# Feed-forward gate and up products of a float32 network: pairs of feature blocks in seven block products instead of eight, and the down product in four groups

## The chip, the core and the metric

The kernel runs on one core of a Trainium2 chip. The metric is the device time of one launch in microseconds (us), median of several runs. Five engines work on their own instruction rows, each in order: PE (TensorE) multiplies matrices, DVE (VectorE) and ACT (ScalarE) do the element-wise work, POOL (GpSimd) takes some of it, and SP (SyncE) issues most DMA transfers. Engines wait for one another through semaphores.

## The reference

Two blocks of two layers each act on 512 tokens of 1024 features, in float32. What matters here is the feed-forward part at the end of each layer of the second block: a norm, two products to 2816 features (gate and up), a convolution over three tokens on the gate, silu, the product of both, and a product back to 1024 features.

```python
# first block, two layers: x = x + rms_norm(mixed(rms_norm(x)) @ w_out)
...
for l in range(DEPTH):
    hn = rmsnorm(h, norm_mix[l])
    if l % 2 == 0:
        h = h + even_mixer(hn, ...)
    else:
        h = h + odd_mixer(hn, ...)
    h = h + conv_ffn(rmsnorm(h, norm_ffn[l]), ffn_w_up[l], ffn_w_gate[l],
                     ffn_conv_w[l], ffn_conv_b[l], ffn_w_down[l])
return rmsnorm(h, norm_final)[:, N_META:N_META + S]

def conv_ffn(h, w_up, w_gate, conv_w, conv_b, w_down):
    u = h @ w_up
    g = h @ w_gate
    g = lax.conv_general_dilated(g, ...) + conv_b
    return (jax.nn.silu(g) * u) @ w_down
```

In layer 0 there are 528 tokens (16 meta tokens and 512 of x). In layer 1 only the 512 tokens of x are wanted, and for the gate 4 tokens ahead of them, 516 columns in all.

## The kernel before

Activations lie with features on partitions, in blocks (or chunks) of 128, and tokens in columns. A float32 product runs as three passes: weights and activations are each split exactly into a high and a low part, and `dense()` issues, for each chunk k of the contraction, high times high, high times low and low times high (L165). 528 columns take two PSUM banks, so each pass is two matmuls of 264 columns; 516 columns are two of 258.

`weights()` loads 512 KB or less by SP (tile `wr`, L148), copies the high part on ACT (`wh`, L149) and subtracts on DVE to get the low part (`wl`, L150). The pool holds 2 tiles `wr`, 4 `wh` and 4 `wl`. `split()` does the same to activations (L155, L156). `Norm.part` makes the operand of a norm's products: X times the gain, high on ACT (L68) and low on DVE (L69), and sums squares (L232, L235); the statistics of each token pass through PE (L242, `ps_ss`, and L259, `ps_rs`), and the result `rs` multiplies products as they leave PSUM.

`ffn()` goes through the 22 feature blocks in three groups of 8, 7 and 7. For a block it makes the gate product and the up product (8 chunks of contraction each, 48 matmuls each in layer 0; in layer 1 the up product is 24 matmuls of 512 columns). The gate takes `rs` on DVE as it leaves PSUM (tile `g`, L1077), then ACT (`z`, L1078), two convolution steps on DVE (L1080), silu on ACT (L1081), z times `rs` on POOL (L1082), z times the up product on DVE (L1083), and the split into `aH` and `aL`. After a group, `added()` multiplies its chunks with the down weights: for each of 8 output blocks one product of 7 or 8 chunks, added to X on DVE (L694). The last group of layer 1 goes through `final()`, which works by halves of the tokens and ends with the last norm and the output.

The program is written in this order; a scheduler that estimates times, and the limited tiles of each pool, set in what order each engine's instructions stand in the end. The row of each engine is then fixed and is worked off in order.

## Time and profile before

| | |
|---|---|
| median of three runs | 2132.17 us (2124.72, 2132.17, 2137.76) |
| profiled execution, its span | 2134.1 us |
| PE busy | 2066.6 us, 97% |
| DVE, ACT, POOL busy | 58%, 41%, 26% |
| feed-forward layer 0, unbroken matmuls | 380.94 us |
| feed-forward layer 1, unbroken matmuls | 337.98 us |

The profile is of one execution. Its own time is the span; nothing outside it is recorded for that execution. The feed-forward parts are some 34% of the span. A line number such as L165 is one of the kernel before; the changed kernel's lines are one higher up to `ffn()`, and its own from there on.

### The profile page before, as it was taken

How to read it: one execution, taken by the hardware profiler on the slowest of the kernel's cores; microseconds unless marked ns; L12 is line 12 of the kernel's file. 1: busy time of each engine (PE TensorE's matmuls, PEld its weight loads, DVE VectorE, ACT ScalarE, POOL GpSimd, SP SyncE). 2: the span in 40 equal slices, each digit the busy share in tenths (PEclk: the TensorE clock that was granted, in tenths of full speed). 3: DMA queues.
4: the chain of work that ended last, by engine and by line, in shares of the span. 5: the costliest groups of instructions: out<-in, count | busy, mean ns of one | idle time of the engine just before them, and what ended most of it. 6: DMA issues, size and time to landing. Idle time of an engine off the chain costs nothing.

```text
span 2134.1 us, 36059 instructions
## 1 busy us (share of the span) xinstructions
PE 2066.6 (97%) x14456; PEld 1888.8 (89%) x14456; DVE 1228.9 (58%) x2016; ACT 865.7 (41%) x1543; POOL 544.9 (26%) x652
## 2 busy tenths in 40 slices
PE   8999999999989999999999999999999999999998
PEld 6788888788789899988999999999888899888898
DVE  5565756665666896545554354454665665444454
ACT  5455644455644322344333232334433444223233
POOL 2222223222235555364010010001445401000001
PEclk9999999999999999999999999999999999999999
DMA  6633224633224323343222223234342233322322
GB/s 202 182 106 106 65 87 132 167 105 99 65 75 121 89 80 98 113 129 83 79 99 90 90 86 94 90 90 115 106 121 76 81 106 99 95 94 82 106 84 75
DMA packets 75590, 216.49 MB, mean 101 GB/s; under 512 B 10936, under 2 KB 15056, under 8 KB 75424
## 3 DMA queue, kind: packets, MB, share of 16 engines
q1 hardware_dynamic: 71792, 205.93, 33.3%
q0 software_dynamic: 2336, 7.19, 1.2%
q8 instruction: 114, 1.87, 0.4%
q10 hardware_dynamic: 1296, 1.09, 0.2%
q14 instruction: 52, 0.43, 0.1%
HBM read 166.20 MB, written 6.92 MB: 81 GB/s over the span
## 4 chain that ended last, share of the span: by engine, by line
PE 83%; DVE 7%; DMA 4%; issue 2%; SPq 1%; ACT 1%; POOL 1%; DVEq 0%; POOLq 0%; ACTq 0%
PE ps_mm L165 66%; PE ps_s L372 2%; PE ps_t L379 2%; PE ps_o L469 2%; PE ps_out L165 1%; DMA ks<-st 1%; PE ps_o L984 1%; PE ps_o L412 1%; PE ps_z L1034 1%; DVE yo L579 1%; DVE wl L150 1%; PE ps_t L956 1%; DMA sq<-t 1%; PE ps_ro L863 1%; DVE s L1037 1%
## 5 line engine op out<-in xcount | busy, mean ns | idle before, releaser
L165 PE MATMUL ps_mm<-hH,wh 128*128 128x264 f32 (+3 forms) x2712 | 677.0, 312 | 18.2 <-DVE t L189 7.5
L165 PE MATMUL ps_mm<-hL,wh 128*128 128x264 f32 (+3 forms) x2712 | 679.6, 311 | 10.8 <-DVE hL L69 10.8
L165 PE MATMUL ps_mm<-hH,wl 128*128 128x264 f32 (+3 forms) x2712 | 678.1, 311 | 0.0
L149 ACT ACTIVATE wh<-wr 128x1024 fp32r<-128x1024 f32 (+3 forms) x301 | 301.5, 1003 | 633.8 <-PE ps_mm L165 573.9
L165 PEld LDWEIGHTS ps_mm<-hH,wh 128*128 128x128 f32 x2712 | 448.6, 190 | 47.0 <-DVE t L189 7.7
L165 PEld LDWEIGHTS ps_mm<-hL,wh 128*128 128x128 f32 x2712 | 448.4, 190 | 35.7 <-DVE hL L69 12.5
L165 PEld LDWEIGHTS ps_mm<-hH,wl 128*128 128x128 f32 x2712 | 448.7, 190 | 25.6 <-issue 1.4
L150 DVE TENSOR_TENSOR wl<-wr,wh 128x1024 fp32r<-128x1024 f32 (+3 forms) x277 | 330.9, 1196 | 99.1 <-ACT wh L149 89.4
L1082 POOL TENSOR_TENSOR z<-z,rs 128x528 f32<-128x528 f32 (+1 forms) x44 | 58.1, 1322 | 601.6 <-ACT z L1081 601.6
L694 DVE TENSOR_TENSOR X<-X,ps_mm 128x528 f32<-128x528 f32 (+2 forms) x72 | 50.2, 697 | 156.1 <-PE ps_mm L165 155.7
L165 PE MATMUL ps_mm<-aL,wh 128*128 128x264 f32 (+2 forms) x528 | 134.4, 310 | 0.0
L165 PE MATMUL ps_mm<-aH,wl 128*128 128x264 f32 (+2 forms) x528 | 134.2, 309 | 0.0
L165 PE MATMUL ps_mm<-aH,wh 128*128 128x264 f32 (+2 forms) x528 | 133.9, 309 | 0.0
L189 DVE TENSOR_TENSOR t<-ps_mm,rs 128x528 f32<-128x528 f32 (+1 forms) x101 | 70.1, 695 | 85.1 <-PE ps_mm L165 79.6
L1077 DVE TENSOR_TENSOR g<-ps_mm,rs 128x528 f32<-128x528 f32 (+1 forms) x44 | 30.8, 701 | 119.9 <-PE ps_mm L165 119.9
L165 PE MATMUL ps_mm<-yH,wh 128*128 128x264 f32 (+2 forms) x392 | 95.3, 309 | 0.2 <-DVE X L694 0.2
L165 PE MATMUL ps_mm<-yH,wl 128*128 128x264 f32 (+2 forms) x392 | 94.6, 307 | 0.0
L165 PE MATMUL ps_mm<-yL,wh 128*128 128x264 f32 (+2 forms) x392 | 93.8, 305 | 0.0
L165 PEld LDWEIGHTS ps_mm<-aL,wh 128*128 128x128 f32 x528 | 87.6, 188 | 5.6
L165 PEld LDWEIGHTS ps_mm<-aH,wl 128*128 128x128 f32 x528 | 87.5, 188 | 5.5
L165 PEld LDWEIGHTS ps_mm<-aH,wh 128*128 128x128 f32 x528 | 87.2, 188 | 5.6
L1083 DVE TENSOR_TENSOR z<-z,ps_mm 128x528 f32<-128x528 f32 (+1 forms) x44 | 30.6, 695 | 87.8 <-PE ps_mm L165 48.6
(268 smaller groups left out, 3198.4 us busy)
## 6 DMA issues: line engine op xcount, KB each, us to landing
wr<-w1c SPq DMA_DIRECT2D x52, 512.0 KB, 3.9
wr<-gate SPq DMA_DIRECT2D x44, 512.0 KB, 3.4
wr<-up SPq DMA_DIRECT2D x44, 512.0 KB, 3.4
ks<-st SPq DMA_DIRECT2D x48, 264.0 KB, 5.4
wr<-down SPq DMA_DIRECT2D x28, 448.0 KB, 3.4
wr<-we_b SPq DMA_DIRECT2D x24, 512.0 KB, 3.7
wr<-wo_c SPq DMA_DIRECT2D x24, 512.0 KB, 3.8
qs<-st SPq DMA_DIRECT2D x64, 132.0 KB, 3.4
```

The lines of the kernel that those rows point to most:

```text
L149: nc.scalar.activation(high, raw, AF.Copy)
L150: getattr(nc, eng).tensor_tensor(low, raw, high.bitcast(F32), op=OP.subtract)
L165: self.nc.tensor.matmul(p[:a.shape[2]], a[:, k], b[k][:, t], start=bool(first and k == 0 and j == 0), stop=bool(last and k == len(ah) - 1 ...
L189: self.nc.vector.tensor_tensor(f(out), v, f(r), op=OP.mult)
L372: nc.tensor.matmul(ps, qs[:, c, 128 * i:128 * i + 128], ks[c][:, j], start=j == 0, stop=j == 1)
L379: nc.tensor.transpose(pt[:, 128 * k:128 * k + 128], src[:, 128 * k:128 * k + 128], self.ident)
L412: nc.tensor.matmul(oi, aT[:, 128 * k:128 * k + 128], va[:, 128 * k:128 * k + 128], start=k == 0, stop=k == 3)
L469: nc.tensor.matmul(po[64 * c:64 * c + 64, 128 * i:128 * i + 128], BV[:, 128 * k + 64 * c:128 * k + 64 * c + 64], pT[c][:, 128 * k:128 * k ...
L694: self.nc.vector.tensor_tensor(f(x[:, o]), f(x[:, o]), v, op=OP.add)
L1077: nc.vector.tensor_tensor(two(g[:, lead - u:]), vg, two(rs), op=OP.mult)
L1082: nc.gpsimd.tensor_tensor(z, z, rs[:, u:], op=OP.mult)
L1083: nc.vector.tensor_tensor(f(z), f(z), vu, op=OP.mult)
```

## The change

Block i and block i + 11 of the gate (and of the up) product are made together. Their weights and the activations are seen as matrices of 2 by 2 blocks: two blocks of features, two halves of the contraction (chunks 0 to 3, and 4 to 7), two halves of the columns. `paired()` makes the four results from seven block products instead of eight, by sums of weights (tiles `ws`, L1170, four additions of 128x512 on DVE for each pair and product) and sums of activations that `seven()` makes once at the start. A block product is 4 chunks by 3 passes on half the columns, 12 matmuls of 264 (or 258) columns.

The seven are written in the order 1, 5, 6, 2, 7, 4, 3. Products 1, 6, 7 and 4 are accumulated one on another in one PSUM bank (`ps_a`, two tiles). After 1, 6 and 7 ACT copies what stands in it (L1198 and L1201 into the halves of `g` or `u`, L1204 into `f`). Products 2 and 5 go to the two banks of a tile `ps_mm` (`pb`, `pc`), and 3 is added to `pc` after DVE has added `pc` to `f` (L1205). The results of block i are `g` (or `u`) plus both banks (L1208); those of block i + 11 are minus `f` and minus `ps_a`, which DVE takes with the multiplication by `rs` (L1094, L1095) or by z (L1099, L1100). All weights are split on chip: `wr` and two tiles of sums, 1024 columns each, and one half, `wy`, of 512.

The steps of a block from `g` to `aH` and `aL` are as before, for two blocks at a time. The groups are 3, 3, 3 and 2 pairs, so the down product runs in four groups of 6, 6, 6 and 4 chunks; the host lays the down weights out in that order. The products ahead of each ffn write the blocks of X in the order of PAIRS, so that chunk k and chunk k + 4 come one behind the other. In layer 1 the up product is now made for 516 columns.

The core of the diff:

```diff
     def ffn(self, l, out=None):
         nc, d = self.nc, self.d
         X, n, u = (self.X, T2, 0) if l == 0 else (self.X[:, :, TAIL:], S, NM - TAIL)
-        lead = u or 2
-        self.tb = (2, 1)[l]
-        self.mm = (3, 2)[l]
-        up = {} if l == 0 else dict(a=u, tag="u", bufs=3)
-        down = dict(up)
-        down.pop("a", 0)
-        f = two if n > S else lambda x: x
+        lead, w = u or 2, n + u
+        m = w // 2
+        self.tb, self.mm = 2, 2
         with ExitStack() as c:
-            pp = Banks(self.tc, c, "ffn", ("t mm2 mm0 mm1", "t u mm0 mm1")[l])
+            pp = Banks(self.tc, c, "ffn", "mm1 t a mm0")
             fp = c.enter_context(self.tc.tile_pool(name="ffn", bufs=1))
-            new = lambda n, w, bufs, dt=F32: fp.tile([128, w], dt, name=n, tag=n, bufs=bufs)
+            new = lambda name, cols, bufs, dt=F32: fp.tile([128, cols], dt, name=name, tag=name, bufs=bufs)
             cw = fp.tile([128, 22, 4], F32, name="cw")
             nc.gpsimd.dma_start(cw, d[f"conv_{l}"])
-            h, rs = self.normed(pp, X, self.gain[:, 6 + l], [d[f"gate_{l}"][0], d[f"up_{l}"][0]], [{}, up])
-            for a, b in ((0, 8), (8, 15), (15, 22)):
-                act = [], []
+            ops, rs = self.seven(pp, fp, X, self.gain[:, 6 + l])
+            act = [], []
+            def activated(i, g):
+                z = new("z", n, 4)
+                nc.scalar.activation(z, g[:, lead:], AF.Identity, scale=cw[:, i, 2:3], bias=cw[:, i, 3:4])
+                for k in range(2):
+                    nc.vector.scalar_tensor_tensor(z, g[:, lead - 2 + k:lead - 2 + k + n], cw[:, i, k:k + 1], z, op0=OP.mult, op1=OP.add)
+                nc.scalar.activation(z, z, AF.Silu)
+                nc.gpsimd.tensor_tensor(z, z, rs[:, u:], op=OP.mult)
+                return z
+            def done(z):
+                act[0].append(new("aH", n, 7, F32R))
+                act[1].append(new("aL", n, 7, F32R))
+                self.split(act[0][-1], act[1][-1], z)
+            for a, b in ((0, 3), (3, 6), (6, 9), (9, 11)):
+                act[0].clear()
+                act[1].clear()
                 for i in range(a, b):
-                    vg = self.product(pp, d[f"gate_{l}"][i], h)[1]
-                    vu = self.product(pp, d[f"up_{l}"][i], h, **up)[1]
-                    g, z = new("g", lead + n, 2), new("z", n, 3)
+                    g = [new("g", lead + n, 3) for _ in range(2)]
                     if u == 0:
-                        nc.vector.memset(g[:, :2], 0.0)
-                    nc.vector.tensor_tensor(two(g[:, lead - u:]), vg, two(rs), op=OP.mult)
-                    nc.scalar.activation(z, g[:, lead:], AF.Identity, scale=cw[:, i, 2:3], bias=cw[:, i, 3:4])
-                    for k in range(2):
-                        nc.vector.scalar_tensor_tensor(z, g[:, lead - 2 + k:lead - 2 + k + n], cw[:, i, k:k + 1], z, op0=OP.mult, op1=OP.add)
-                    nc.scalar.activation(z, z, AF.Silu)
-                    nc.gpsimd.tensor_tensor(z, z, rs[:, u:], op=OP.mult)
-                    nc.vector.tensor_tensor(f(z), f(z), vu, op=OP.mult)
-                    act[0].append(new("aH", n, 16, F32R))
-                    act[1].append(new("aL", n, 16, F32R))
-                    self.split(act[0][-1], act[1][-1], z)
-                if out is None or b < 22:
-                    self.added(pp, d[f"down_{l}"], act, a, b, X[:, :, u:], **down)
+                        for t in g:
+                            nc.vector.memset(t[:, :2], 0.0)
+                    e = g[0][:, lead - u:]
+                    f, t = self.paired(pp, fp, d[f"gate_{l}"], i, ops, e, m)
+                    nc.vector.tensor_tensor(e, e, rs, op=OP.mult)
+                    nc.vector.scalar_tensor_tensor(g[1][:, lead - u + m:], f, -1.0, rs[:, m:], op0=OP.mult, op1=OP.mult)
+                    nc.vector.scalar_tensor_tensor(g[1][:, lead - u:lead - u + m], t, -1.0, rs[:, :m], op0=OP.mult, op1=OP.mult)
+                    z = [activated(i + 11 * j, g[j]) for j in range(2)]
+                    e = new("u", w, 2)
+                    f, t = self.paired(pp, fp, d[f"up_{l}"], i, ops, e, m)
+                    nc.vector.scalar_tensor_tensor(z[1][:, m - u:], f, -1.0, z[1][:, m - u:], op0=OP.mult, op1=OP.mult)
+                    nc.vector.scalar_tensor_tensor(z[1][:, :m - u], t[:, u:], -1.0, z[1][:, :m - u], op0=OP.mult, op1=OP.mult)
+                    nc.vector.tensor_tensor(z[0], z[0], e[:, u:], op=OP.mult)
+                    for t in z:
+                        done(t)
+                if out is None or b < 11:
+                    self.added(pp, d[f"down_{l}"], act, 2 * a, 2 * b, X[:, :, u:])
                 else:
-                    self.final(pp, fp, d[f"down_{l}"], act, a, b, out)
+                    self.final(pp, fp, d[f"down_{l}"], act, 2 * a, 2 * b, out)
+    def seven(self, pp, fp, x, g):
+        nc, w = self.nc, x.shape[2]
+        m = w // 2
...
+        sums = self.sums(pp, w, 8)
+        ops = [([], []) for _ in range(4)]
+        for k in range(4):
+            j = k + 4
+            x1, x2, gk, gj = x[:, k], x[:, j], g[:, k:k + 1], g[:, j:j + 1]
+            h, l = (first[i][k // 2][:, m * (k % 2):m * (k % 2) + m] for i in range(2))
+            nc.scalar.activation(h, x1[:, :m], AF.Copy, scale=gk)
+            nc.vector.scalar_tensor_tensor(l, x1[:, :m], gk, h.bitcast(F32), op0=OP.mult, op1=OP.subtract)
+            ops[0][0].append(h)
+            ops[0][1].append(l)
+            b12 = fp.tile([128, T2], F32, name="z", tag="z", bufs=4)[:, :m]
+            nc.scalar.activation(b12, x1[:, m:], AF.Copy, scale=gk)
+            s = [fp.tile([128, T2], F32, name="g", tag="g", bufs=3)[:, :w] for _ in range(2)]
+            t1, t2, t3, t4 = s[0][:, :m], s[0][:, m:], s[1][:, :m], s[1][:, m:]
+            nc.vector.scalar_tensor_tensor(t1, x1[:, :m], gk, b12, op0=OP.mult, op1=OP.subtract)
+            h, l = more(), more()
+            nc.scalar.activation(h, x2, AF.Copy, scale=gj)
+            nc.vector.scalar_tensor_tensor(l, x2, gj, h.bitcast(F32), op0=OP.mult, op1=OP.subtract)
+            ops[1][0].append(h)
+            ops[1][1].append(l)
+            nc.vector.scalar_tensor_tensor(t2, x2[:, m:], ng[:, j:j + 1], t1, op0=OP.mult, op1=OP.subtract)
+            nc.vector.scalar_tensor_tensor(t3, x2[:, m:], gj, b12, op0=OP.mult, op1=OP.subtract)
+            nc.vector.scalar_tensor_tensor(t4, x2[:, :m], ng[:, j:j + 1], t2, op0=OP.mult, op1=OP.subtract)
+            for i in range(2):
+                h, l = more(), more()
+                self.split(h, l, s[i])
+                ops[2 + i][0].append(h)
+                ops[2 + i][1].append(l)
+            sums(x1)
+            sums(x2)
+        lo, hi = slice(0, m), slice(m, w)
+        cols = lambda i, c: [[t[:, c] for t in part] for part in ops[i]]
+        right = {1: ops[0], 2: cols(1, lo), 3: cols(1, hi), 5: cols(2, lo), 6: cols(2, hi), 7: cols(3, lo), 4: cols(3, hi)}
+        rs = self.row_tile("rs", w)
+        for out, a, b in self.rstd(pp, sums, 1.0 / D):
+            nc.scalar.activation(rs[:, a:b], out, AF.Copy)
+        return right, rs
+    def paired(self, pp, fp, src, i, right, e, m):
+        nc, wp = self.nc, self.wp
+        raw = [(wp if j == 0 else fp).tile([128, 1024], F32, name="wr", tag="wr", bufs=2) for j in range(2)]
+        for j in range(2):
+            nc.sync.dma_start(raw[j].rearrange("p (k n) -> p k n", n=128), src[i + 11 * j])
+        half = lambda t: (t[:, :512], t[:, 512:])
+        (a11, a12), (a21, a22) = half(raw[0]), half(raw[1])
+        s13, s24 = (fp.tile([128, 1024], F32, name="ws", tag="ws", bufs=2) for _ in range(2))
+        (s1, s3), (s2, s4) = half(s13), half(s24)
+        for o, p, q in ((s1, a21, a22), (s3, a11, a21), (s2, a11, s1), (s4, a12, s2)):
+            nc.vector.tensor_tensor(o, p, q, op=OP.add)
+        own = lambda n: wp.tile([128, 1024], F32R, name=n, tag=n, bufs=self.wb[1])
+        new = lambda n, b: fp.tile([128, 1024], F32R, name=n, tag=n, bufs=b)
+        left = {}
+        def parts(high, low, x, keys):
+            self.split(high, low, x)
+            for key, h, l in zip(keys, half(high), half(low)):
+                left[key] = [t.rearrange("p (k n) -> p k n", n=128) for t in (h, l)]
+        parts(own("wh"), own("wl"), raw[0], (1, 2))
+        parts(own("wh"), own("wl"), s13, (5, 7))
+        parts(new("wx", 3), new("wx", 3), s24, (6, 3))
+        h, l = half(new("wy", 1))
+        self.split(h, l, a22)
+        left[4] = [t.rearrange("p (k n) -> p k n", n=128) for t in (h, l)]
+        pa = pp.tile([128, 512], F32, name="ps_a", tag="a", bufs=2)[:, :m]
+        pt = pp.tile([128, 2, 512], F32, name="ps_mm", tag="mm", bufs=2)
+        pb, pc = pt[:, 0, :m], pt[:, 1, :m]
+        def product(ps, j, start=False):
+            (wh, wl), (bh, bl) = left[j], right[j]
+            for k in range(4):
+                for v, (p, q) in enumerate(((wh, bh), (wh, bl), (wl, bh))):
+                    nc.tensor.matmul(ps, p[:, k], q[k], start=start and k == 0 and v == 0, stop=k == 3 and v == 2, skip_group_check=not start)
+        f = fp.tile([128, T2 // 2], F32, name="f", tag="f", bufs=2)[:, :m]
+        product(pa, 1, True)
+        nc.scalar.activation(e[:, :m], pa, AF.Copy)
+        product(pc, 5, True)
+        product(pa, 6)
+        nc.scalar.activation(e[:, m:], pa, AF.Copy)
+        product(pb, 2, True)
+        product(pa, 7)
+        nc.scalar.activation(f, pa, AF.Copy)
+        nc.vector.tensor_tensor(f, f, pc, op=OP.add)
+        product(pa, 4)
+        product(pc, 3)
+        nc.vector.tensor_tensor(two(e), two(e), pt[:, :, :m], op=OP.add)
+        return f, pa
```

In the operand numbers, `right[1]` is the first half of the contraction at the first half of the columns, `right[2]` and `right[3]` the second half of the contraction, and 5, 6, 7 and 4 are the sums `s[0]` and `s[1]`.

On ACT, before, in the middle of layer 0's gate and up products (`wh` is a weight copy, `z` and `aH` belong to a block's steps):

```order
L155 ACTIVATE aH<-z 128x528 [waits DVE_49]
L149 ACTIVATE wh<-wr 128x1024 [waits DMAHW2_49,PE_49,Activation_49]
L1078 ACTIVATE z<-g,cw 128x528 [waits DVE_49]
L1081 ACTIVATE z<-z 128x528 [waits DVE_49]
L149 ACTIVATE wh<-wr 128x1024 [waits DMAHW3_49,PE_49,Activation_49]
L155 ACTIVATE aH<-z 128x528 [waits DVE_49]
L149 ACTIVATE wh<-wr 128x1024 [waits DMAHW4_49,PE_49,Activation_49]
L1078 ACTIVATE z<-g,cw 128x528 [waits DVE_49]
L1081 ACTIVATE z<-z 128x528 [waits DVE_49]
```

And after, in the same place:

```order
L156 ACTIVATE wh<-wr 128x1024 [waits DMAHW0_49,PE_49]
L1204 ACTIVATE f<-ps_a 128x264 [waits PE_49]
L1074 ACTIVATE z<-z 128x528 [waits DVE_49] x2
L156 ACTIVATE wy<-wr 128x512 [waits DMAHW3_49,PE_49,Activation_49]
L1198 ACTIVATE u<-ps_a 128x264 [waits PE_49]
L1201 ACTIVATE g<-ps_a 128x264 [waits PE_49]
L156 ACTIVATE aH<-z 128x528 [waits DVE_49]
L156 ACTIVATE aH<-z 128x528 [waits Pool_49]
L156 ACTIVATE wx<-ws 128x1024 [waits DVE_49]
L156 ACTIVATE wh<-ws 128x1024 [waits DVE_49,PE_49]
L156 ACTIVATE wh<-wr 128x1024 [waits DMAHW2_49,PE_49]
L1204 ACTIVATE f<-ps_a 128x264 [waits PE_49]
```

The copy `f`, which PE waits for, now stands behind weight copies that wait for PE themselves. The last one ahead of it waits for the second-to-last matmul of product 7, and `f` for the last.

On PE, before, the end of a group's last up product and the first down matmul (the 96 matmuls of a block have no more in their rows than the first three here):

```order
L165 MATMUL ps_mm<-hH,wh 128x264 x2
L165 MATMUL ps_mm<-hL,wh 128x264 x2
L165 MATMUL ps_mm<-hH,wl 128x264 x2
L165 MATMUL ps_mm<-aH,wh 128x264 [waits DMASW0_49,DVE_49,Activation_49]
L165 MATMUL ps_mm<-aH,wh 128x264
```

After, from the end of a product 7 through 4 and 3 to the start of the next 1 (tiles: `wh` and `wl` with `ps_a` are product 7, `wx` with `ps_a` product 6 of the next pair, `wy` product 4, `wx` with `ps_mm` product 3):

```order
L1194 MATMUL ps_a<-op,wh 128x264 x2
L1194 MATMUL ps_a<-op,wl 128x264
L1194 MATMUL ps_a<-h,wx 128x264 [waits Activation_49]
L1194 MATMUL ps_a<-h,wx 128x264
L1194 MATMUL ps_a<-h,wy 128x264 [waits Activation_49]
L1194 MATMUL ps_a<-h,wy 128x264 x5
L1194 MATMUL ps_a<-op,wy 128x264 x6
L1194 MATMUL ps_mm<-h,wx 128x264 [waits DVE_49]
L1194 MATMUL ps_mm<-h,wx 128x264 x5
L1194 MATMUL ps_mm<-op,wx 128x264 x6
```

Between 7 and 4 stand two matmuls of another product, and 4 waits for ACT, 3 for DVE.

On DVE, before, one block's row in layer 0:

```order
L1077 TENSOR_TENSOR g<-ps_mm,rs 128x528 [waits PE_49]
L150 TENSOR_TENSOR wl<-wr,wh 128x1024 [waits DMAHW2_49,Activation_49]
L1080 SCALAR_TENSOR_TENSOR z<-g,cw,z 128x528 [waits Activation_49]
L1080 SCALAR_TENSOR_TENSOR z<-g,cw,z 128x528 [waits DVE_49]
L1076 MEMSET g 128x2 [waits DVE_49]
L1083 TENSOR_TENSOR z<-z,ps_mm 128x528 [waits PE_49,Pool_49]
L150 TENSOR_TENSOR wl<-wr,wh 128x1024 [waits DMAHW3_49,Activation_49]
L156 TENSOR_TENSOR aL<-z,aH 128x528 [waits Activation_49]
```

After, from the end of a gate product to the addition to `f` of the up product that follows:

```order
L1208 TENSOR_TENSOR g<-g,ps_mm 128x528 [waits PE_49]
L1170 TENSOR_TENSOR ws<-wr,ws 128x512 [waits DVE_49]
L1093 TENSOR_TENSOR g<-g,rs 128x528 [waits DVE_49]
L1170 TENSOR_TENSOR ws<-wr,ws 128x512 [waits DVE_49]
L1170 TENSOR_TENSOR ws<-wr 128x512 [waits DMAHW7_49]
L1170 TENSOR_TENSOR ws<-wr 128x512
L1073 SCALAR_TENSOR_TENSOR z<-g,cw,z 128x528 [waits Activation_49] x2
L1073 SCALAR_TENSOR_TENSOR z<-g,cw,z 128x528 [waits DVE_49] x2
L157 TENSOR_TENSOR wl<-ws,wh 128x1024 [waits PE_49,Activation_49]
L1090 MEMSET g 128x2 [waits DVE_49] x2
L157 TENSOR_TENSOR wl<-wr,wh 128x1024 [waits DMAHW0_49,PE_49,Activation_49]
L1205 TENSOR_TENSOR f<-f,ps_mm 128x264 [waits Activation_49]
```

Ahead of them stands one more weight subtraction (L157, `wx`), which waits for the end of the gate's product 3. Where 8 rows made up a block, these rows and that one (16 instructions) stand between the end of a gate product and the addition that lets the up product's 3 write to `pc`.

## Rows read from the trace of the kernel before

**Rows 1.** The page: busy time of each engine, granted clock by slices.

```profile
PE 2066.6 (97%) x14456; PEld 1888.8 (89%) x14456; DVE 1228.9 (58%) x2016; ACT 865.7 (41%) x1543; POOL 544.9 (26%) x652
...
PEclk9999999999999999999999999999999999999999
```

**Rows 2.** The chain that ended last: start us, us, what, number of instructions.

```profile
289.96 11.88 PE ps_out L165 x99
...
1080.54 380.94 PE ps_mm L165 x3116
...
1767.03 337.98 PE ps_mm L165 x2003
...
1074.84 1.01 PE ps_ss L242 x10
...
1079.95 0.59 PE ps_rs L259 x5
```

**Rows 3.** Windows: us, busy time of each engine, granted clock, DMA share, GB/s.

```profile
1080.00:1460.00 380.00, 380.00 (x3111) 379.80 (x3110) 185.35 (x238) 124.29 (x152) 33.82 (x32) 1.00 0.29 92
1767.00:2105.00 338.00, 338.00 (x2007) 298.96 (x2006) 165.25 (x206) 114.17 (x150) 28.94 (x22) 1.00 0.30 91
945.00:980.00 35.00, 31.40 (x246) 29.02 (x245) 22.18 (x49) 20.06 (x43) 22.46 (x37) 0.97 0.54 145
```

**Rows 4.** Timeline of DVE in layer 0: start us, us, instruction [idle before].

```profile
1109.30 0.71 DVE L1077 TENSOR_TENSOR g<-ps_mm,rs 128x528 f32<-128x528 f32 x1 [3.10 <-PE ps_mm L165]
...
1132.85 0.71 DVE L1077 TENSOR_TENSOR g<-ps_mm,rs 128x528 f32<-128x528 f32 x1 [3.15 <-PE ps_mm L165]
```

**Rows 5.** Timeline of DVE in layer 1.

```profile
1801.05 0.69 DVE L1077 TENSOR_TENSOR g<-ps_mm,rs 128x516 f32<-128x516 f32 x1 [3.06 <-PE ps_mm L165]
...
1823.73 0.69 DVE L1077 TENSOR_TENSOR g<-ps_mm,rs 128x516 f32<-128x516 f32 x1 [3.02 <-PE ps_mm L165]
```

**Rows 6.** Timeline of PE in layer 1.

```profile
1774.52 0.41 PE L165 MATMUL ps_mm<-hL,wh 128*128 128x258 f32 x2
...
1775.96 0.28 PE L165 MATMUL ps_mm<-hL,wh 128*128 128x258 f32 x1
```

**Rows 7.** Groups of ACT in layer 0: count, busy us, mean ns, idle before.

```profile
L149 ACT ACTIVATE wh<-wr 128x1024 fp32r<-128x1024 f32 x51 | 54.1, 1061 | 155.2 <-PE ps_mm L165 155.2
...
L149 ACT ACTIVATE wH<-wr 128x512 fp32r<-128x512 f32 x4 | 2.5, 632 | 3.0 <-DMA wr<-down 3.0
```

**Rows 8.** The end of the chain.

```profile
2127.30 0.45 PE ps_rs L259 x2
...
2127.82 0.39 ACT rs L1111
```

**Rows 9.** Groups of DVE in layer 0 and layer 1, and two in a row.

```profile
L150 DVE TENSOR_TENSOR wl<-wr,wh 128x1024 fp32r<-128x1024 f32 x52 | 63.9, 1231 | 15.6 <-ACT wh L149 11.9
L1080 DVE SCALAR_TENSOR_TENSOR z<-g,cw,z 128x528 f32<-128x528 f32 x44 | 34.1, 776 | 3.1 <-ACT z L1078 2.4
...
L694 DVE TENSOR_TENSOR X<-X,ps_mm 128x528 f32<-128x528 f32 x24 | 16.9, 704 | 69.7 <-PE ps_mm L165 69.7
...
L1105 DVE TENSOR_TENSOR X<-X,ps_mm 128x256 f32<-128x256 f32 x8 | 3.2, 415 | 1.6 <-PE ps_mm L165 1.6
L150 DVE TENSOR_TENSOR wL<-wr,wH 128x512 fp32r<-128x512 f32 x4 | 2.8, 692 | 5.3 <-ACT wH L149 3.3 <-PE ps_mm L165 2.0
...
1079.27 2.36 DVE L150 TENSOR_TENSOR wl<-wr,wh 128x1024 fp32r<-128x1024 f32 x2 [7.54 <-ACT wh L149]
```

**Rows 10.** Timelines of POOL and DVE where they overlap.

```profile
1088.67 1.32 POOL L1082 TENSOR_TENSOR z<-z,rs 128x528 f32<-128x528 f32 x1 [11.24 <-ACT z L1081]
1092.62 1.34 POOL L1082 TENSOR_TENSOR z<-z,rs 128x528 f32<-128x528 f32 x1 [2.62 <-ACT z L1081]
...
1089.35 1.21 DVE L1080 SCALAR_TENSOR_TENSOR z<-g,cw,z 128x528 f32<-128x528 f32 x1 [1.45 <-ACT z L1078]
...
1093.52 1.52 DVE L150 TENSOR_TENSOR wl<-wr,wh 128x1024 fp32r<-128x1024 f32 x1 [0.91 <-ACT wh L149]
```

More of the change, by code (lines that the diff above doesn't have):

```diff
@@ L682, in parted, with added @@
         e.tensor_tensor(o[:, :, low], x, o[:, :, 0].bitcast(F32), op=OP.subtract)
-    def added(self, pp, src, act, a, b, x, **opts):
+    def added(self, pp, src, act, a, b, x, order=range(8), **opts):
         m = 6 if b - a > 8 else b - a
@@ L689, in added @@
         f = two if n > S else lambda x: x
-        for o in range(8):
+        for o in order:
             _, ps, v = self.bank(pp, 0, n, **opts)
@@ L1092, in final @@
     def final(self, pp, fp, src, act, a, b, out):
         nc, x, m = self.nc, self.X[:, :, NM:], S // 2
-        W = [[(0, b - a, self.weights(src[o, :, a:b]))] if o < 4 else
-             [(k, e, self.weights(src[o, :, a + k:a + e], True)) for k, e in ((0, 4), (4, b - a))] for o in range(8)]
+        W = [[(0, b - a, self.weights(src[o, :, a:b], o >= 4))] for o in range(8)]
+        rows = [fp.tile([128, T2], F32, name="o", tag="op", bufs=12) for _ in range(8)]
         for i in range(2):
             c = slice(m * i, m * i + m)
-            sums, y = self.sums(pp, m, 8, 1), []
+            sums, y = self.sums(pp, m, 8, 1), [t[:, c] for t in rows]
```

15 lines of the change are left out of this document (10 added, 5 removed).

## The prediction

> **What bounds the kernel now.** I read the page first: TensorE (PE) is busy 97% of the span (2134.1 us), VectorE (DVE) 58%, ScalarE (ACT) 41%, and the row PEclk stands at 9 or more throughout [rows 1]. Then the chain that ended last: its longest pieces are the feed-forward products, 380.94 us of L165 without a break in layer 0 and 337.98 us in layer 1 [rows 2]. The windows of the two stretches say the same: PE busy 380.00 of 380 and 338.00 of 338 at a granted clock of 1.00 (its 2.4 GHz level), with DVE at 185.35 and 165.25 us, about half [rows 3]. So there every matmul taken away is time, and everything that makes PE wait is new time: the stretch holds no idle PE into which a wait could fall. A block of features (gate and up, 96 matmuls in layer 0) takes 11.775 us, two of them 23.55 [rows 4], which is 0.1227 us per matmul of 264 columns; in layer 1 two blocks take 22.68 [rows 5].
>
> **What is removed.** A pair of blocks had 192 matmuls in layer 0 and has 2 x 84 = 168. The new ones change the stationary operand with each matmul, as those of ps_out in the chain do (99 in 11.88 us, 0.120 each at 256 columns [rows 2]), so no price is added for that: 168 x 0.1227 = 20.6, a saving of 2.94 a pair, 32.4 in 11. In layer 1 the up product had 24 matmuls of 512 columns, and six pairs of 258 take 1.44 [rows 6]: 168 x 0.1205 = 20.24 against 22.68, 26.8 in 11. **Saved: 59.2 us.** One product (seven block products) is then 84 x 0.1227 = 10.3 us of PE.
>
> **What is added on ACT, on the path.** Block products 1, 6, 7 and 4 accumulate in one bank, ps_a, and after each of the first three ACT must have read it before PE may add the next. In the order, the copy f (L1204) between 7 and 4 stands right behind a weight copy (L156) of the next product, and that copy waits on PE: its buffer is read last by the second-to-last matmul of this same 7. This is so at all 44 f copies: the copy ahead has 1024 columns at 20 of them, 768 at 18, 512 at 6. Between 7 and 4 PE has only two matmuls of another product in its row (0.25 us) at 30 of the 44, none at the 8 group ends, and 13 or 14 (1.6 us) at the first product of the 6 groups that follow another within a layer; PE runs in order. So but for those 6 PE stands still for the weight copy, the f copy and the way there and back, less 0.25. The weight copy of 1024 columns takes 1.061, of 512 0.632 [rows 7]; 768 lies between at 0.85. A copy of 256 columns out of PSUM took 0.39 [rows 8]. The hand-overs I take at 0.15 in all, an estimate: in the chain ACT starts 0.07 after the matmul's end [rows 8], and a matmul ends 0.16 later than the next one starts (0.28 against 0.12 [rows 6]), of which the last matmul of 7 covers 0.12. Gaps: 1.35, 1.14 and 0.92 us; 20 x 1.35 + 18 x 1.14 + 6 x 0.92 = 53, less 6 x 1.2 for the covered ones: **+46**. The low end, without the hand-overs, is 41; the high end, 0.1 more each, 51. Less than nothing is excluded: an added wait of an in-order engine cannot end its work sooner. The copies after 1 and 6 cost nothing: ten matmuls of another product (1.2 us) or whole products stand behind them.
>
> **What is added on DVE.** A gate product's end, a chain on DVE starts: between the last reads of one product's PSUM and the addition f+=pc (L1205) of the next, without which its block product 3 may not overwrite pc, stand 16 instructions: 3 of 1024 columns at 1.23, 4 convolution steps at 0.776, four sums of 512 at 0.69, g*rs and g+=ps at 0.70, f+= at 0.42 [rows 9], and two small memsets. They make 11.4 us. Neighbours overlap by some 0.07 (two of 1231 ns took 2.36 [rows 9], 0.10 less), which leaves 10.4; and two POOL products of 1.33 us run beside them [rows 10]. Where such a product overlapped a DVE instruction with two operands in SBUF, a convolution step of 0.776 took 1.21 and a subtraction of 1.23 took 1.52 [rows 10], +0.43 and +0.29. With 0.7 for both: f is ready after 11.1, product 3 (12 matmuls, 1.47) and a hand-over of 0.1 follow, 12.67 from sync to sync against 10.3 + 1.35 = 11.65 on PE. So here DVE is late by 1.0 us. There are 22 such places, 8 of them at a group's end (next term): **14 x 1.0 = +14** (4 if the POOL overlap costs nothing). From up to gate there is less on DVE (14 or 15 instructions, 9.1 to 10.2 us by the same prices), so PE leads; DVE frees ps_a about 0.3 late, **+4** (0 to 8). In sum a pair takes 12.65 + 11.95 = 24.6 us against 23.55 before: so with its waits a pair of seven products is longer than one of eight.
>
> The Trainium skill ("SBUF — State Buffer", section "Who interferes with whom") says that a DVE instruction with two SBUF inputs and a GpSimd instruction that reads SBUF exclude each other for a whole instruction. The two overlaps above agree in sign, with 0.43 and 0.29 us for 0.64 and 0.44 us of overlap. By the rule two products could block DVE for 2 x 1.33 us instead of the 0.7 that I take; that is the second rival.
>
> **Group ends.** With four groups there are eight. Behind the last pair there is no next product in PE's row to fill with, the z steps stand ahead of the weight and f copies on ACT (1.061 and 0.39, some 1.45), and the first down matmul waits for z, u and the split, of which about 1.0 is not covered: 8 x 2.4 = **+19**. Low 8, if only the z steps show; high 28.
>
> **Start of each ffn.** Before, the norm was 15 instructions on DVE and PE had products to do meanwhile; the chain has only the statistics, 1.01 + 0.59 us [rows 2]. Now seven() makes four operand sets. After the last X addition 26 DVE instructions stand ahead of the last operand: 2 x 1.23, 9 x 0.70, 8 steps of 264 columns at 0.44 (between 0.42 at 256 and 0.776 at 528), 4 sums at 0.69, 3 memsets. They make 15.1, or 13.5 with overlaps, while PE has 54 matmuls, 6.6 us, that don't need them. Ahead of that, 45 instructions between the last nine X additions make 27.0 to 30.1 against PE's 25.1, so DVE may already be 1.9 to 5.0 behind. 13.5 - 6.6 - 1.6 (statistics, PE's own, which fall into the gap) = 5.3 at least, 13 at most a start; I take 7.5, since the last operands are needed only by the last block products: 2 x 7.5 = **+15** (10 to 26).
>
> **At nothing.** The fourth down group adds 16 X additions of 0.704 us on DVE [rows 9], 11 us under 288 down matmuls a group (35.3 us, DVE 34 at most): hidden, and the cost is the excess of DVE if it isn't. Gate and up loads stay 512 KB each, as many as before, and are issued a product ahead. The final part on four chunks instead of seven leaves the end of the chain as it is.
>
> **The sum.** -59.2 + 46 + 14 + 4 + 19 + 15 = +38.8. On the profiled span, 2172.9; that execution lies 1.9 us above the median of the three runs (2132.17), so 2171. All low ends give -59.2 + 41 + 4 + 0 + 8 + 10 = +4, 2136; all high ends, with DVE locked half the time, -59.2 + 51 + 32 + 8 + 28 + 26 = +86, 2218.
>
> **Rivals.** First, a gain: the waits at f are hidden. It needs that the weight copy is ready to go early, so that ACT reaches f when 7 ends. Then only the f copy and hand-overs less 0.25 remain, 0.3 us x 38 = 11, DVE keeps up, and with starts and group ends at their low ends -59 + 11 + 18 = -30 to, with nothing but the starts at 15, -44: 2088 to 2102. It decides at (59.2 - 15 - 19)/38 = 0.66 us per product. For it speaks that DVE and ACT have half their time free [rows 3]; against it that the copy's buffer is PE's own, read up to the end of 7. 0.08. Second, DVE as the bound: two POOL products lock it for 2.65 us a pair instead of 0.7, +2.0 at 22 places = 44: 2215. Against it are the two overlaps, which cost two thirds of their length [rows 10]. 0.10. Third, the clock: PE at 100% had 1.00; a window with PE at 90% (31.40 of 35) had 0.97 [rows 3]. If gaps of 5 to 8% pull the clock down by 3% over some 750 us, +22: 2193. Against it: that window lies in another part, with DMA and POOL far busier. 0.07. Fourth, that the change is as slow as worked out only at its low ends, 2128 to 2153: 0.19. The forecast, 2153 to 2205, has the rest, 0.56.
>
> **How the numbers follow.** A measurement of this kernel tells about 1% from no change (its three runs span 0.6%): 2111 to 2153. Faster 0.08 from the first rival, same 0.19 from the fourth, slower 0.73 from the rest. The range leaves out the gain and what lies above the high ends; below it goes 8 us past the low ends, since the gain's price shades into them: 2128 to 2218.
>
> **What would show it.** In the changed profile: PE's busy share in the two stretches near 90% instead of 100%, with idle ahead of L1194 matmuls of 7-to-4 released by ACT f, about 1.1 us each 38 times, and ahead of product 3 by DVE f; two gate products 24 to 25 us apart; PE idle some 7 us at each ffn start behind DVE; the parts before the first ffn unchanged. Wrong would be: f copies that start as product 7 ends, DVE over 95% busy between the products, or a clock under 0.95 there.

## The result and the profile after

| | median | runs |
|---|---|---|
| before | 2132.64 us | 2124.72 to 2137.76 |
| changed | 2214.82 us | 2210.51 to 2218.26 |

The ratio is 1.0392, 95% interval 1.0356 to 1.0428: slower by 82 us where 39 was forecast. The time lies at the upper end of the range (2128 to 2218) and above the forecast (2153 to 2205). The profiled spans are 2215.0 and 2134.1 us, 80.9 apart.

The page of the changed kernel, against [rows 1]:

```profile
PE 2052.8 (93%) x14384; PEld 1865.7 (84%) x14384; DVE 1488.5 (67%) x2490; ACT 986.6 (45%) x1799; POOL 554.2 (25%) x652
...
PEclk9999999999999999999999999999999989999999
```

PE has less to do and a longer span; DVE has gained 260 us, ACT 121. Windows of the changed kernel, against [rows 3]: a group's products in layer 0, its down product, then 10 us at the start of each ffn:

```profile
1100.00:1160.00 60.00, 48.90 (x379) 46.56 (x378) 48.27 (x78) 30.30 (x47) 9.43 (x6) 1.00 0.29 93
1160.00:1195.00 35.00, 34.69 (x286) 34.48 (x285) 21.42 (x28) 10.98 (x13) 0.00 (x0) 1.00 0.29 98
...
1070.00:1080.00 10.00, 7.01 (x33) 6.00 (x32) 10.00 (x18) 3.45 (x6) 0.00 (x0) 0.66 0.00 0
...
1795.00:1805.00 10.00, 7.62 (x41) 6.67 (x41) 8.90 (x17) 5.03 (x10) 1.33 (x1) 0.67 0.15 52
```

The down product is nearly as full as before (34.69 of 35). PE's pauses lie between the products (48.90 busy of 60) and at the starts, where DVE is busy for 10.00 and 8.90 of 10 us and the granted clock, which has two levels (1.00 is 2.4 GHz, 0.50 is 1.2 GHz), averages 0.66 and 0.67. The waits of PE in the whole span (us in total, times, longest):

```profile
PE ps_a L1194 <- ACT f L1204: 37.0, 38, 1.7
PE ps_a L1194 <- DVE z L1100: 23.5, 14, 2.4
...
PE ps_a L1194 <- DVE wx L157: 8.9, 8, 1.2
...
PE ps_mm L166 <- DVE u L1208: 5.7, 7, 0.8
```

Each wait is 0.16 longer between starts of matmuls than the table says, since a matmul's shown end lies that much behind the next one's start [rows 6]: 43 us for f, 25.7 for z, 10.2 for wx. On the timeline of PE, one pair in layer 0:

```profile
1117.73 0.41 PE L1194 MATMUL ps_a<-h,wx 128*128 128x264 f32 x2
1119.20 0.99 PE L1194 MATMUL ps_a<-h,wy 128*128 128x264 f32 x6 [1.06 <-ACT f L1204]
...
1135.75 0.51 PE L1194 MATMUL ps_a<-h,wh 128*128 128x264 f32 x2 [1.70 <-DVE z L1100]
...
1148.57 0.75 PE L1194 MATMUL ps_a<-h,wx 128*128 128x264 f32 x4 [1.20 <-DVE wx L157]
```

The wait for f is the one foretold: the first row is the two matmuls of another product, then PE stands until the copy is through. The wait for z was foretold at 0.3 a time. Its chain runs over three engines; the timelines of ACT, POOL and DVE ahead of 1135.75:

```profile
1129.38 0.84 ACT L150 ACTIVATE wh<-wr 128x768 fp32r<-128x768 f32 x1 [0.40 <-PE ps_a L1194]
1130.13 0.37 ACT L1204 ACTIVATE f<-ps_a 128x264 f32<-128x264 f32 x1
1130.40 1.17 ACT L1074 ACTIVATE z<-z 128x528 f32<-128x528 f32 x2
...
1131.11 3.77 POOL L1075 TENSOR_TENSOR z<-z,rs 128x528 f32<-128x528 f32 x2 [21.41 <-ACT z L1074]
...
1134.92 0.43 DVE L1099 SCALAR_TENSOR_TENSOR z<-f,z 128x264 f32<-128x264 f32 x1 [1.19 <-POOL z L1075]
1135.27 0.42 DVE L1100 SCALAR_TENSOR_TENSOR z<-ps_a,z 128x264 f32<-128x264 f32 x1
```

Weight copy, f copy, two silus, two products on POOL, then L1099 and L1100, the last reader of ps_a: 6.3 us in a row, and only then may the next block product 1 write that bank. The POOL group, where [rows 10] had 1.32 to 1.34:

```profile
L1075 POOL TENSOR_TENSOR z<-z,rs 128x528 f32<-128x528 f32 x22 | 35.5, 1629 | 345.9 <-ACT z L1074 345.9
```

Pairs in one group of layer 0, by DVE's g*rs, against [rows 4]: 25.4 and 24.5 us where two blocks took 23.55.

```profile
1210.24 0.70 DVE L1093 TENSOR_TENSOR g<-g,rs 128x528 f32<-128x528 f32 x1
...
1235.64 0.70 DVE L1093 TENSOR_TENSOR g<-g,rs 128x528 f32<-128x528 f32 x1
...
1260.14 0.71 DVE L1093 TENSOR_TENSOR g<-g,rs 128x528 f32<-128x528 f32 x1
```

### The profile page after: what moved, and what is told of

Same layout as the page of the kernel before. It is cut to its first block, busy times and chain, and to the rows that moved or that the text cites. A ratio compares the mean times of both kernels' runs of the same rounds, so it can differ in the third digit from the quotient of the medians.

```text
span 2215.0 us, 36664 instructions
## 1 busy us (share of the span) xinstructions
PE 2052.8 (93%) x14384; PEld 1865.7 (84%) x14384; DVE 1488.5 (67%) x2490; ACT 986.6 (45%) x1799; POOL 554.2 (25%) x652
## 3 DMA queue, kind: packets, MB, share of 16 engines
q8 instruction: 113, 1.85, 0.3%
## 5 line engine op out<-in xcount | busy, mean ns | idle before, releaser
L166 PE MATMUL ps_mm<-hH,wh 128*128 128x264 f32 (+3 forms) x1480 | 393.5, 323 | 18.7 <-DVE t L190 7.6
L166 PE MATMUL ps_mm<-hL,wh 128*128 128x264 f32 (+3 forms) x1480 | 396.0, 321 | 10.8 <-DVE hL L70 10.8
L166 PE MATMUL ps_mm<-hH,wl 128*128 128x264 f32 (+3 forms) x1480 | 394.6, 320 | 0.0
L150 ACT ACTIVATE wh<-wr 128x1024 fp32r<-128x1024 f32 (+3 forms) x229 | 212.0, 929 | 321.3 <-PE ps_mm L166 243.0
L151 DVE TENSOR_TENSOR wl<-wr,wh 128x1024 fp32r<-128x1024 f32 (+3 forms) x205 | 229.2, 1121 | 85.0 <-ACT wh L150 81.2
L166 PEld LDWEIGHTS ps_mm<-hH,wh 128*128 128x128 f32 (+1 forms) x1480 | 250.2, 192 | 39.5 <-DVE t L190 7.8
L166 PEld LDWEIGHTS ps_mm<-hL,wh 128*128 128x128 f32 (+1 forms) x1480 | 251.6, 192 | 28.9 <-DVE hL L70 12.5
L166 PEld LDWEIGHTS ps_mm<-hH,wl 128*128 128x128 f32 (+1 forms) x1480 | 251.8, 192 | 17.9 <-issue 1.4
L1075 POOL TENSOR_TENSOR z<-z,rs 128x528 f32<-128x528 f32 (+1 forms) x44 | 68.6, 1574 | 689.8 <-ACT z L1074 689.8
L1194 PE MATMUL ps_a<-h,wh 128*128 128x264 f32 (+1 forms) x528 | 105.6, 293 | 27.1 <-DVE z L1100 23.5
L1194 PEld LDWEIGHTS ps_a<-h,wh 128*128 128x128 f32 x528 | 84.7, 194 | 32.6 <-issue 13.6
```

What stands on the lines that cost most here:

```text
L150: nc.scalar.activation(high, raw, AF.Copy)
L151: getattr(nc, eng).tensor_tensor(low, raw, high.bitcast(F32), op=OP.subtract)
L166: self.nc.tensor.matmul(p[:a.shape[2]], a[:, k], b[k][:, t], start=bool(first and k == 0 and j == 0), stop=bool(last and k == len(ah) - 1 ...
L1075: nc.gpsimd.tensor_tensor(z, z, rs[:, u:], op=OP.mult)
L1194: nc.tensor.matmul(ps, p[:, k], q[k], start=start and k == 0 and v == 0, stop=k == 3 and v == 2, skip_group_check=not start)
```

## The experiments

The theory: PE waits for three things in turn, f, z (which holds ps_a) and wx, and at each start for operands. The rivals: DVE is the bound, so that a wait taken away comes back elsewhere; or the clock does it. Ratios are against the kernel before on the same chip and occasion (2128.9 to 2134.7 us); a gain told below is a difference of two ratios times 2133 us.

| run | edit to the changed kernel | median us | ratio, interval |
|---|---|---|---|
| 1 | weight copies behind f | 2206.57 | 1.0334 (1.0307 to 1.0362) |
| 2 | copy of ps_a on ACT | 2214.21 | 1.0372 (1.0334 to 1.0410) |
| 3 | no z*rs on POOL | 2185.84 | 1.0245 (1.0211 to 1.0279) |
| 4 | no sums of activations | 2192.17 | 1.0265 (1.0235 to 1.0295) |
| 5 | 1 and 2, four wx | 2155.99 | 1.0128 (1.0109 to 1.0147) |
| 6 | no sums of weights | 2189.58 | 1.0284 (1.0268 to 1.0300) |
| 7 | kernel before, four down groups | 2134.83 | 1.0027 (1.0013 to 1.0041) |
| 8 | 5, sums of weights on POOL | 2216.59 | 1.0417 (1.0400 to 1.0435) |
| 9 | 1, four wx | 2170.49 | 1.0165 (1.0143 to 1.0187) |
| 10 | 2, four wx | 2158.71 | 1.0119 (1.0092 to 1.0146) |
| 11 | 5, squares summed on PE | 2181.30 | 1.0222 (1.0196 to 1.0247) |
| 12 | 11, first weight sums on POOL | 2177.10 | 1.0204 (1.0180 to 1.0227) |
| 13 | four wx alone | 2158.85 | 1.0129 (1.0086 to 1.0173) |
| 14 | 10, no sums of activations | 2136.48 | 1.0005 (0.9991 to 1.0020) |
| 15 | 10, later weight sums at the start | 2148.77 | 1.0075 (1.0047 to 1.0104) |

**Run 1: the weight copies stand behind f.** `fc` collects the copies f, and `issue_after` puts what it encloses behind one of them. The copies of the down weights are moved in the same way (not printed).

```diff
+        behind = lambda k: self.tc.issue_after(self.fc[-k].ins) if len(self.fc) >= k else ExitStack()
...
-        parts(own("wh"), own("wl"), raw[0], (1, 2))
-        parts(own("wh"), own("wl"), s13, (5, 7))
+        with behind(2):
+            parts(own("wh"), own("wl"), raw[0], (1, 2))
+            parts(own("wh"), own("wl"), s13, (5, 7))
...
-        nc.scalar.activation(f, pa, AF.Copy)
+        self.fc.append(nc.scalar.activation(f, pa, AF.Copy))
```

> The changed kernel, with the weight copies on ScalarE queued behind the copy f that they stood in front of; nothing else. In the changed kernel's trace matmuls wait 43 us for f. Theory (the weight copy in front of f is what they wait for): the copy f itself, 0.37 us, and the hand-overs stay, less the 0.25 us of two other matmuls, so 0.3 us at 38 places: 43 falls to 11, and the kernel to some 2183 us. Rival (the waits only move: the silus now stand behind two more weight copies, and the second part of z, which frees ps_a, comes later): matmuls wait for that instead, 27 us become 45 to 60, and the time stays within 10 us of 2215.

PE's waits in its trace:

```profile
PE ps_a L1199 <- DVE wx L157: 41.7, 24, 2.4
PE ps_mm L166 <- DVE u L1213: 16.2, 8, 2.4
...
PE ps_a L1199 <- ACT f L1209: 7.6, 24, 0.5
```

The wait for f went as the theory said, 37.0 to 7.6, so the weight copy in front was its cause. The time fell by 12 only: the rival's form was right, its place not; wx took over, not z. The clock took a part too. Between the products of layer 1 it averaged 0.97, where the changed kernel has 1.00 (1840 to 2180 us), and in layer 0 (1100 to 1480 us) 0.99 instead of 1.00; both together are some 15 us short of full speed:

```profile
1810.00:2180.00 370.00, 335.12 (x2217) 307.36 (x2216) 283.06 (x389) 155.75 (x241) 40.44 (x22) 0.97 0.28 85
```

**Run 2: ps_a is freed by a copy on ACT.**

```diff
-                    f, t = self.paired(pp, fp, d[f"up_{l}"], i, ops, e, m)
+                    f, pa = self.paired(pp, fp, d[f"up_{l}"], i, ops, e, m)
+                    t = g[1][:, 2:2 + m]
+                    nc.scalar.activation(t, pa, AF.Copy)
```

> The changed kernel, with the last reading of ps_a of each up product done by a copy on ScalarE right after block product 4, so that ps_a need not wait for z, which comes through GpSimd; VectorE then takes z from the copy. Theory (ps_a is held until GpSimd's two products of z and rs are through): the 14 waits for z, 27 us, go, at a price of 0 to 5 us for the copies: some 2190 us. Rival (VectorE is late there anyway, by its own row of work): matmuls wait a little later for wx or f on VectorE instead, and under 8 us are gained.

```profile
PE ps_a L1196 <- ACT f L1206: 37.4, 38, 1.6
PE ps_a L1196 <- DVE wx L157: 25.7, 22, 1.2
...
PE ps_a L1196 <- ACT g L1100: 8.5, 14, 1.0
```

4 us less, no more than the intervals leave open. The wait for z is gone, 25.7 for wx and 8.5 for the new copy stand in its place: the rival's result, but in the main not by its reason. At 13 of the 22 waits for wx DVE was not behind with its row: it had itself stood idle for PE's block product 3, as here ahead of a wait of 1.20 us:

```profile
1142.56 1.23 DVE L157 TENSOR_TENSOR wx<-ws,wx 128x1024 fp32r<-128x1024 f32 x1 [0.20 <-PE ps_mm L1196]
```

**Run 3: z*rs is left out.** The line L1075 goes.

> The changed kernel without the multiplication of z by rs on GpSimd, which is left out of the computation. Theory (the chain silu, GpSimd, z holds ps_a): the 27 us go as in the copy's run, 2188 us. If the two products on GpSimd also slow VectorE by 0.3 to 0.4 us each, 22 more places gain 0.7 us or part of it, down to 2175. Rival (VectorE's own row is the cause): above 2205.

31 us less. Waits for z are gone, and f and wx stay at 38.2 and 9.2 us. DVE's convolution steps took 763 ns as with POOL's products beside them (761), so the gain is not from a faster DVE: it is POOL's part of the chain.

**Run 4: no sums of activations.** The four t-steps, the copy b12 and both splits of s are left out (24 DVE and 12 ACT instructions a start; the counts in the expectation are too high):

```diff
...
             for i in range(2):
-                h, l = more(), more()
-                self.split(h, l, s[i])
                 ops[2 + i][0].append(h)
                 ops[2 + i][1].append(l)
```

> The changed kernel without the sums of activations at the start of each ffn: the two operand sets of sums are left out and the second half's set stands in for them, so 36 VectorE instructions and 20 of ScalarE less a start and as many matmuls. Theory (operands late at the start, and the clock that falls in that gap): the 17 us of waits for operands fall to 3 to 5, and the granted clock, 0.66 to 0.83 in the 10 us windows there, goes back to 1.00, 10 us or more: 2185 to 2190 us. Rival (the clock falls for the statistics or for the waits between products, and not for the late operands): 12 us are gained, 2203.

The window of the start, where the changed kernel had 7.01 and 0.66:

```profile
1070.00:1080.00 10.00, 9.69 (x80) 9.45 (x80) 6.56 (x9) 4.78 (x9) 1.19 (x1) 1.00 0.18 52
```

27 us less: late operands and the clock that fell with them. It is at 1.00 in the 10 us windows of both starts.

**Run 5: both edits and a fourth buffer for wx.** aH and aL give up one of seven buffers each; runs 8 to 15 have this too.

```diff
-        parts(new("wx", 3), new("wx", 3), s24, (6, 3))
+        parts(new("wx", 4), new("wx", 4), s24, (6, 3))
```

> The changed kernel with the first two edits together (weight copies behind f; ps_a freed by a copy on ScalarE) and a fourth buffer for wx (aH and aL have six buffers each instead of seven). The two edits alone gave 8 and 1 us, since VectorE's wx came late in their place (10 us of waits became 45 and 29). Theory (wx is late because its buffer is freed only by the block product 3 of the product before, so that VectorE makes it at the last moment): with a fourth buffer each wait goes for itself, f 43 to 11, z 27 to 11, wx 45 to 5 or 10, and the time falls by 45 to 55 to some 2165 us. Rival (VectorE has 20 us of work a pair, as much as the matmuls, 20.6, and any wait taken away comes back at VectorE's row): 2190 to 2200.

56 us less, the time that the theory of single causes forecast: the wait for f is 3.8 us, those for z and for DVE's wx are gone. Runs 9, 10 and 13 test whether it is for that theory's reason.

**Run 6: no sums of weights.** The four additions go, and both parts are made of the second block's weights.

> The changed kernel without the sums of weights: VectorE's 176 additions of 512 columns are left out, some 0.62 us each, and the parts are made of the second block's weights as they are. Everything else stands. If VectorE's load is what makes z and wx late: their 27 and 10 us go by half or more, and with f's 43 kept the time is some 2190 us. If the waits come from the order of the steps and from GpSimd alone: within 8 us of 2215.

23 us less with f at 37.8: the wait for z fell from 23.5 to 7.8, wx kept its 8.9. POOL's products took 1380 ns instead of 1629 in layer 0. So DVE's load is a part of what made z late; whether by its own row, which is shorter ahead of the convolution steps here, or through POOL, this run does not separate.

**Run 7: four groups in the kernel before.**

```diff
-            for a, b in ((0, 8), (8, 15), (15, 22)):
+            for a, b in ((0, 6), (6, 12), (12, 18), (18, 22)):
```

The last group's down weights are cut to four chunks to match (not printed).

> The kernel before, with eight block products as it was, and four groups of 6, 6, 6 and 4 chunks in the down product. The prediction had this at nothing: the further X additions are hidden under the down matmuls. By it 2133 us, 5 either way. Rival (a group's end costs by itself, as it does in the changed kernel, some 12 us over eight): 2137 to 2145.

6 us slower, 3 to 9 by the interval: small, but not the nothing of the prediction, and within the rival's 4 to 12.

**Run 8: sums of weights on GpSimd.** One word of run 5, `nc.vector` to `nc.gpsimd`.

> The kernel of the first run above (three edits) with the sums of weights on GpSimd instead of VectorE, eight of 512 columns a pair, some 1.3 us each there. If VectorE's load is what is left: 5 us a pair are free, the pair comes near its 20.6 us of matmuls, and the time is 20 to 30 us under that run. If GpSimd and VectorE hold each other up (two products of z that take 1.33 us alone took 1.6 on average in the changed kernel), z comes later than before and the time is no lower than that run's, or higher by 10 or more.

The groups of POOL, and DVE's convolution steps, in layer 0:

```profile
L1175 POOL TENSOR_TENSOR ws<-wr 128x512 f32<-128x512 f32 x38 | 61.9, 1645 | 164.7 <-DMA wr<-up 66.1 <-DVE X L697 59.7 <-DVE wx L157 14.6
...
L1078 POOL TENSOR_TENSOR z<-z,rs 128x528 f32<-128x528 f32 x22 | 40.6, 1853 | 48.8 <-ACT z L1077 48.8
...
L1076 DVE SCALAR_TENSOR_TENSOR z<-g,cw,z 128x528 f32<-128x528 f32 x44 | 50.8, 1199 | 4.7 <-ACT z L1074 4.7
```

62 us slower than run 5: the products of z take 1.85 us and queue behind the sums, DVE's convolution steps beside them take 1199 ns where the changed kernel had 761, and the clock averages 0.96 between the products (run 5: 0.99). So the two engines do hold each other up here, as the second theory had it.

**Runs 9, 10 and 13: which of the three edits does it.**

> The changed kernel with the weight copies behind f and four buffers for wx, without the copy that frees ps_a. If the wait for wx, which took the place of the wait for f (45 us), came from its buffer alone: 8 + 30 to 35 are gained against the changed kernel, 2170 to 2178. If z holds ps_a there (silu stands behind two more weight copies on ScalarE, so z is later than it was): the 45 us become a wait for z of 35 to 50, and the time stays at 2200 to 2210. The two together then explain why the three edits gave 59 and each alone next to nothing.

> The changed kernel with the copy that frees ps_a and four buffers for wx, the weight copies left in front of f. The wait for f, 43 us, must stay. If the wait for wx (29 us with the copy alone) came from its buffer: it falls to 5 or so, 25 are gained, 2190. If VectorE's load makes wx late whatever its buffers: 2210.

> The changed kernel with four buffers for wx (six for aH and aL) and nothing else: no order forced, no copy of ps_a. The run with copy and four wx lost the wait for f too, from 43 us to 8, though nothing was asked of f: with the further buffer the scheduler put other work in front of it. If the buffer does that alone: f falls to 10 or so, z stays at 27 to 40, and the time is 2175 to 2185. If it took the copy of ps_a to bring the new order about: f stays at 40 and the time is 2205 to 2215.

Run 9 came out as its first forecast. In run 10 the wait for f, which had to stay, fell to 6.6 us; in run 13 f fell as forecast, and z, which had to stay, fell too. The fourth buffer, with one less for aH and aL, gives alone what run 5's three edits give (1.0129 and 1.0128). What the smaller number for aH and aL does by itself was not run. PE's waits in run 13:

```profile
PE ps_a L1194 <- ACT f L1204: 12.6, 13, 1.6
...
PE ps_a L1194 <- DVE z L1100: 4.2, 2, 2.2
```

With three buffers the low part of the next product's wx waits for block product 3 of the present one. With four it is made earlier, and with it the scheduler changed ACT's row: a copy to `wh` stands right in front of f at 20 of 44 places, not at all 44. In run 10 it is 17. A window between the products of run 13 shows what is left:

```profile
1195.00:1245.00 50.00, 48.02 (x385) 47.04 (x384) 48.43 (x75) 29.05 (x43) 5.79 (x4) 1.00 0.29 96
```

PE 96%, DVE 97%: between the products of a group DVE is now as full as PE. Over the whole of layer 0's groups (1100 to 1460 us) it is 80%, PE 94%. Forcing the order as well (run 9) gained nothing more (1.0165).

**Runs 11 and 12: less DVE at the start.** The squares of X are summed by one-column matmuls (`self.sums(pp, w, 8, 8)`); in run 12 the first two products' sums of weights go to GpSimd too.

> The run with three edits (weight copies behind f, copy of ps_a, four wx), and at the start of each ffn the squares are summed by matmuls alone: seven VectorE additions of 528 columns less a start, some 4.3 us, for some 35 small matmuls more, 3.5 us where the matmuls wait anyway. If VectorE's row of 26 instructions is what the start waits for: 4 us a start and 1 to 2 of the clock, some 10 in all, so 2146. Rival (the statistics, rs, hold the start): 2156, or 2160 with the matmuls' price.

> As the run before it, and the sums of weights of the first two products of each ffn on GpSimd, which is idle there: eight VectorE additions less, another 4.9 us a start. If GpSimd leaves VectorE alone: another 8 to 12 us, 2136. If the eight additions on GpSimd, some 1.3 us each and longer beside VectorE, hold the first products themselves: no gain, or 5 to 10 us lost.

Both lost, 20 and 16 us against run 5. The start of run 11:

```profile
1070.00:1080.00 10.00, 10.00 (x51) 9.90 (x51) 10.00 (x19) 5.97 (x10) 0.00 (x0) 0.52 0.17 52
1080.00:1090.00 10.00, 10.00 (x64) 9.87 (x63) 2.08 (x6) 2.51 (x6) 1.12 (x1) 0.67 0.01 2
1090.00:1100.00 10.00, 10.00 (x67) 9.80 (x66) 3.14 (x4) 3.24 (x6) 0.08 (x1) 0.79 0.00 0
```

PE reads as busy throughout, but at 0.52, 0.67 and 0.79 of the clock for 30 us. In both starts together the clock stood at 0.50 for 51 us, in run 5 for 24; the difference is 14 us of full speed. Neither theory had that.

**Runs 14 and 15: what the start is worth once the waits are gone.**

> The run with the copy of ps_a and four wx (2158.7 us), without the sums of activations at the start of each ffn, as in the fourth run: the two sets of sums are left out and the second half's set stands in. If late operands and the clock in that gap are independent of the waits between the products, the 23 us that they were worth there are gained here too: 2136, the time of the kernel before. If not, as when the first products then wait for VectorE's sums of weights: 2145 to 2155.

> The run with the copy of ps_a and four wx, and at the start of each ffn the weight sums of the second to fourth product queued on VectorE behind the last operand, where VectorE has 6 us without work. Nothing is left out. Six of the instructions ahead of the last operand, some 4 to 5 us a start, come later; with the clock's share 10 to 15 us for both: 2144 to 2150. Rival (the second product then waits for its own weights): no gain, 2155 to 2165.

Without the sums the time is that of the kernel before, 24 us under run 10: the start is a cost of its own. Run 15 queues the sums of the second to fourth product behind the last operand (`np` counts the products, `lastop` is the last subtraction of `seven()`):

```diff
-        for o, p, q in ((s1, a21, a22), (s3, a11, a21), (s2, a11, s1), (s4, a12, s2)):
-            nc.vector.tensor_tensor(o, p, q, op=OP.add)
+        with self.tc.issue_after(self.lastop.ins) if 1 <= self.np < 4 else ExitStack():
+            for o, p, q in ((s1, a21, a22), (s3, a11, a21), (s2, a11, s1), (s4, a12, s2)):
+                nc.vector.tensor_tensor(o, p, q, op=OP.add)
+        self.np += 1
```

By the medians it gets 9 of them back; its interval and run 10's overlap. It is the best full version here, 3.0% under the changed kernel and still 0.75% over the kernel before; none of the runs beats that one.

## Why the prediction was half right

**Right:** the sign and its main cause. f waited at 38 places, the number given, for 43 us between starts where 46 was forecast. Starts cost 15 us in waits for operands and statistics (15 forecast; the waits on h, wh, op, accd, rsm and ACT's wx in both starts, with 0.16 each), the ends of groups 14 (19). A fourth down group, put at nothing, cost 6 in the kernel before (run 7). Two small slips don't matter: [rows 6] give 0.120 us for 258 columns and not 0.1205, 1 us more saved, and at the 8 group ends, where PE has no other matmuls in its row, the 0.25 should not be taken off, 2 us more for f.

**Wrong: the term "DVE frees ps_a about 0.3 late, +4 (0 to 8)".** This is the step that failed. It was 25.7 us, 14 times 1.8. The prediction took only DVE's own row and not the chain that ends there: silu stands behind the f copy on ACT, and the step z waits for both POOL products. That step of the prediction put their cost on DVE: 0.7 us in the chain to f+=, "DVE is late by 1.0", 14 us. The wait for f+= came to 1.1 us in all, so that term was wrong too, by 13 the other way. DVE's steps were not longer (761 ns, [rows 9] 776); POOL's products were (1629 ns on average, up to 2038), and the chain through them ends at ps_a. Run 3 shows it: without POOL's products z is gone from the waits. The Trainium skill ("SBUF — State Buffer", section "Who interferes with whom") says: "Issue order, not op shape, decides who blocks." The runs agree in so far as the side that pays changes: GpSimd in the changed kernel, DVE in [rows 10], both in run 8. The prediction's second rival had DVE pay here. Its time, 2215 us, is the one measured, but by luck: what it priced at 44 us, DVE late at f+=, was the 1.1. With fewer two-operand steps on DVE (run 6) z's wait fell by 16 us.

**Left out of the sum: the clock.** It had a chance of 0.07 as a rival, in the gaps between products. There it stayed at 1.00 in the changed kernel; in runs 1 and 8 it did fall there. It fell at the two starts: in 5 us windows of 1070 to 1090 and 1785 to 1835 the shares missing from 1.00 add up to 14 us. PE waited in a part of that time; by the starts of its matmuls the slower ones cost 9. Run 4, which ends the late operands, has 1.00 there.

**Left out: wx,** 10.2 us, the first wait to show when another goes. The sum: -59 + 43 (f) + 26 (z) + 10 (wx) + 1 (f+=) + 14 (group ends) + 15 (starts) + 9 (clock) is 59 of the 80.9 us between the spans. Another 10 is a term that nobody had: the first matmul behind a wait takes 0.1 us longer, as the two behind the wait for z show above (0.51 us, and 0.41 for the two ahead of the wait for f), and the two ffns have some 100 waits. The mixer of layer 1, between the two ffns, which the change does not touch, took 3.5 us longer, with the clock at 0.50 for 17 us instead of 7. The other 8 or so are not settled.

**Not foreseen: the cause of the order.** The prediction read the row of ACT as given. Run 13 shows that the buffers made it so: with a fourth for wx (and six for aH and aL), f waits 12.6 us instead of 37.0 and z 4.2 instead of 23.5, and 56 of the 82 us are gone. Run 14 shows that the rest goes with the sums of activations at the starts. Even then seven products only equal eight, and why is open. DVE as the bound was wrong for the changed kernel (48.27 of 60). With four buffers DVE is as full as PE between the products of a group (97% and 96%), but no run shows that it is what holds that form back.
